# Seven half products for eight, in two phases, for the first FFN of six prompt tiles

## The chip, the cores and the metric

The kernel runs on one core of a Trainium2 chip. The metric is the device time of one execution in microseconds (us). Times of single instructions are in nanoseconds or microseconds as the profile gives them. An engine's name stands for its instruction stream: PE is the matrix engine, PEld its weight loads, DVE the vector engine, ACT the scalar engine, POOL is GpSimd, SP issues most DMAs.

## The reference, cut to what matters

One encoder layer is applied with the same weights to a prompt of 1024 tokens and a sample of 256 tokens of width 1024, all in float32:

```python
x = layer_norm(ALPHA * x + 0.5 * swiglu_1(x))          # the first FFN
x = layer_norm(ALPHA * x + mixing(x))                  # S5 and Hyena heads
x = layer_norm(ALPHA * x + 0.5 * swiglu_2(x))          # the second FFN
swiglu(x) = (silu(x @ w_gate) * (x @ w_up)) @ w_down   # 1024 -> 2816 -> 1024
```

## The kernel before

**Precision.** A float32 operand is split into a high and a low half in a reduced float32 type (`split`, L171 and L172: ACT writes the high half, DVE the difference). A product is three matmuls: high by high, high by low, low by high.

**Tiles.** Tokens come in tiles of 128: eight of the prompt, two of the sample. The hidden width of 2816 is cut into 22 columns of 128, each a "pass" `ft` below. The first FFN runs as two generators. `fa` has both sample tiles and prompt tiles 0 and 1. `fb` has prompt tiles 2 to 7, that is 768 tokens, held as chunks of 512 and 256 columns.

**fb before.** `ffn` transposes the tiles (L221) and then, for each pass, makes gate and up (`gate_up`, L298): 8 blocks of the width, 3 matmuls, 2 chunks, 2 matrices, which is 96 matmuls, half of them 512 and half 256 columns wide. After every two passes `down` (L331) multiplies the hidden values by `w_down` and adds to the residual rows (L336, L338). Gate/up of the next pass always stands ahead of the down products, so the two kinds alternate for the whole of `fb`. Hidden values stay in SBUF.

**What runs beside it.** `weave` takes a step of the generator that is furthest behind its share. While `fb` runs, `prep` is woven in. It prepares the S5 scan: `s5_prep` and the tables of `s5_mats` (`cmul`, L421 to L426) and then the matrices of `s5_mats` (L543 on DVE, short matmuls L611 and L623). A `yield` tells how much a step counts for, and the second number in `weave` is the generator's whole weight. The scheduler of the framework then orders each engine's instructions by when they become ready, and by the order in which they were written where several are; on the chip each engine runs its list in order.

**The second FFN of the prompt** already has the other form, at 1024 tokens. `Blocks` keeps the transposed tokens as seven blocks (four sums of them made on POOL, L1292, transposed in `put`, L1305). `GateUp` holds the weights of a pass and their four sums (DVE, L1348). `gated` makes gate and up for two token halves of 512 columns by seven products of 12 matmuls (L1368) instead of eight, combines them on DVE (L1384, L1425, L1433), and writes the hidden values to DRAM. When all 22 passes are done, `Down` reads them back with `w_down` and makes the down products (L1511) in groups of four passes.

Of the kernel before, what the change touches and what calls it, by code (L numbers as in the profile page):

```python
# [13 lines left out]
ALU = mybir.AluOpType  # L14
# [239 lines left out]
def ffn(K, NT, x, xT, wg, wu, wd, lng, lnb, cfg, done):  # L254
# [103 lines left out]
    for n, grp in enumerate(groups):  # L358
        last = n == len(groups) - 1
        for f in grp:  # L360
            if f not in hs:
                hs[f] = gate_up(f)
                yield unit
        if last:
            xT.free()
            wgu.free()
            lnv.append(K.new(2, D))
            load_row(K, lnv[0].v[:, 0], lng)
            load_row(K, lnv[0].v[:, 1], lnb)
        ws = [wdown(f) for f in grp]  # L370
        if last and "tail" in cfg:
# [6 lines left out]
    for b in [lnv[0], rawd, wdn, tmp] + hr + extras:  # L378
        b.free()
# [895 lines left out]
class Blocks:  # L1275
# [5 lines left out]
    def __init__(self, K):  # L1281
        self.K = K
        self.b = {n: (K.newr(4, 512), K.newr(4, 512)) for n in self.NAMES}
        self.tmp = K.ring(1, 4, 512)

    def even(self, a, j, banks):
        for n, c in (("11", 0), ("21", 512)):
            self.put(n, a[:, c:c + 512], j, banks)

    def sums(self, x):  # L1290

        TT = lambda o, a, b: self.K.nc.gpsimd.tensor_tensor(out=o, in0=a, in1=b, op=ALU.subtract)  # L1292
        t = self.tmp.get()
        a2, b1, b2 = x[:, 0, 512:1024], x[:, 1, 0:512], x[:, 1, 512:1024]
        TT(t[:, 0], b1, x[:, 0, 0:512])
        TT(t[:, 1], b2, t[:, 0])
        TT(t[:, 2], b2, b1)
        TT(t[:, 3], a2, t[:, 1])
        return {"22": b2, "t1": t[:, 0], "t2": t[:, 1], "t3": t[:, 2], "t4": t[:, 3]}
# [13 lines left out]
class GateUp:  # L1313
# [6 lines left out]
    def __init__(self, K, wg, wu):  # L1320
        self.K, self.wgu = K, (wg, wu)
        self.raw, self.bufs, self.w = {}, {}, {}
        self.sv, self.loaded = None, 0
# [9 lines left out]

    def parts(self, ft):
        K = self.K
        self.bufs[ft] = bg, bu = K.newr(2, 8, 128), K.newr(2, 4, 128)
        g, u = (self.raw[ft].v[:, i] for i in range(2))
        split(K, g, bg.v[:, 0], bg.v[:, 1])
        split(K, u[:, 4:8], bu.v[:, 0], bu.v[:, 1])
        self.w[ft] = {"g1": bg.v[:, :, 0:4], "g2": bg.v[:, :, 4:8], "u2": bu.v}  # L1340

    def sums(self, ft, second):

        K = self.K
        self.sv = self.sv or K.new(2, 4, 128)
        s = self.sv.v
        g, u = (self.raw[ft].v[:, i] for i in range(2))
        TT = lambda o, a, b, op: K.nc.vector.tensor_tensor(out=o, in0=a, in1=b, op=op)  # L1348
        if second:
            TT(s[:, 0], g[:, 4:8], s[:, 1], ALU.subtract)  # L1350
            TT(s[:, 1], g[:, 0:4], u[:, 0:4], ALU.subtract)
            self.raw.pop(ft).free()
        else:
            self.bufs[ft] += (K.newr(4, 4, 128), K.newr(4, 4, 128))
            TT(s[:, 0], u[:, 0:4], u[:, 4:8], ALU.add)
            TT(s[:, 1], s[:, 0], g[:, 0:4], ALU.subtract)
        b, o = [b.v for b in self.bufs[ft][2:]], 2 * second
        split(K, s, *(v[:, o:o + 2] for v in b))
        for i, n in enumerate((("s1", "s2"), ("s4", "s3"))[second]):
            self.w[ft][n] = [v[:, o + i] for v in b]  # L1360

    def product(self, ft, n, X, ps, first):
        a, b = self.OPS[n]
        w, x = self.w[ft][a], [p.v for p in X.b[b]]
        w = (w[:, 0], w[:, 1]) if a in ("g1", "g2", "u2") else w
        todo = [(d, i, k) for d in range(4) for i, k in ((0, 0), (0, 1), (1, 0))]
        for m, (d, i, k) in enumerate(todo):
            self.K.nc.tensor.matmul(ps, lhsT=w[i][:, d], rhs=x[k][:, d], start=first and m == 0, stop=m == len(todo) - 1,  # L1368
                                    skip_group_check=True)

    def free(self, ft):
        for b in self.bufs.pop(ft):
            b.free()
        self.w.pop(ft)


def gated(K, X, G, hd, ids, begin, spare):
# [5 lines left out]
    tmp, hb = K.ring(4, 512), K.ring(1, 2, 512)  # L1383
# [9 lines left out]
    def p1(ft):  # L1393
        st[ft] = s = {"ps": [K.ps[:, b * 512:b * 512 + 512] for b in ids[ft % 2]], "c1": tmp.get()}
# [48 lines left out]
    p7(0)  # L1443
    for ft in range(NFT):
# [6 lines left out]
        nc.sync.dma_start(out=hd[ft], in_=st.pop(ft)["h"].rearrange("p a t -> p (a t)"))  # L1451
        if ft < END:
# [11 lines left out]
    for r in (tmp, hb, G.sv):  # L1464
        r.free()


class Down:
# [24 lines left out]
    def run(self, x, lng, lnb, ids, done, cut):  # L1493
        K, nc = self.K, self.K.nc
        banks = Banks(K, ids)
        for g, grp in enumerate(self.GROUPS):
# [7 lines left out]
            for s in range(8):  # L1504
                o = s % 2 * 512 + s // 2 * 128
                for dh in range(2):
                    ps = banks.get(512)
                    todo = [(f, a, b) for f in grp for a, b in ((0, 0), (0, 1), (1, 0))]
                    for m, (f, a, b) in enumerate(todo):
                        p = self.p[f]  # L1510
                        nc.tensor.matmul(ps, lhsT=p[a].v[:, 1, o:o + 128], rhs=p[b].v[:, 0, dh * 512:dh * 512 + 512],  # L1511
# [40 lines left out]
def emit(ctx, tc, nc, A, dbg=None):  # L1552
# [5 lines left out]
              "rate": (2048,), "h": (NFT, 128, 1024), "x2": (128, 8, D)}  # L1558
# [76 lines left out]
    fb = ffn1([("prompt", s) for s in range(2, 8)], dict(bg=(0, 1, 2, 3), bd=(4, 5), tail=to_mix, rawd=2), turn1)  # L1635
# [10 lines left out]
    weave((fb, 33), (prep((6, 7)), 165))  # L1646
# [52 lines left out]
    class HyenaSide:  # L1699
# [42 lines left out]
        def prompt(self, ids, ids2, G):  # L1742
# [18 lines left out]
            def turn(j):  # L1761
                X.even(x[j].v[:, 0], j, tb)
                for n, v in X.sums(x[j].v).items():
                    X.put(n, v, j, tb)
                x.pop(j).free()

            for j in range(4):
                for i in range(2):
# [70 lines left out]
    dn = Down(K, g("ffn2_w_down"), scr["h"])  # L1839
# [12 lines left out]
    gated(K, X, G, scr["h"], ((0, 1, 2), (3, 4, 5)), begin, spare)  # L1852
# [5 lines left out]
    dn.run(xr[0], g("ln3_g"), g("ln3_b"), range(8), lambda s: nc.sync.dma_start(out=dst[:, s], in_=xr[0].at(s)), cut)  # L1858
# [32 lines left out]
```

## Time and profile before

| | us |
|---|---|
| median of 3 runs | 2580.35 (2579.68 to 2580.8) |
| the profiled execution, its own time | 2577.73 |
| its span, first to last instruction | 2575.9 |
| `fb`, from its first gate product to the last stretch before its tail | about 515 to 1085 of the span |
| second FFN of the prompt, gate/up in steady state | about 1930 to 2290 of the span |

A row "L338 DVE ... x24 | 16.4, 690 | 14.5" means: line 338 of the kernel, engine, 24 instructions, 16.4 us busy in total, 690 ns each on average, and 14.5 us of idle time of that engine just ahead of them. Durations of neighbours on one engine can overlap a little, so busy time is somewhat under count times mean.

### The profile page before, as it was taken

The page shows a single profiled execution, that of the slowest core. Times are in us where ns is not written, and L with a number is a line of the kernel's source. Part 1 is how long each engine was busy: PE and PEld are TensorE (multiplying, and loading weights), DVE is VectorE, ACT ScalarE, POOL GpSimd, SP SyncE. Part 2 cuts the span into 40 slices and gives each one's busy share as a digit, 9 for nine tenths or more (in the row PEclk, how much of TensorE's full clock was granted, in tenths as well). Part 3 has the DMA queues.
Part 4 walks back from the last instruction along what each step waited for, and adds up shares of the span by engine and source line. Part 5 has one row for each costly group of instructions (what it writes and reads, how often), then busy time and mean ns, then how long its engine had stood idle before and what let it go on. Part 6 is the DMA issues. An engine that isn't in the chain of part 4 may idle for free.

```text
span 2575.9 us, 32676 instructions
## 1 busy us (share of the span) xinstructions
PE 2516.0 (98%) x12833; PEld 2106.8 (82%) x12833; DVE 1809.3 (70%) x3016; ACT 812.6 (32%) x1218; POOL 74.7 (3%) x58
## 2 busy tenths in 40 slices
PE   8999999999999999999999999999989999999998
PEld 6767888888888888887888878998768888887887
DVE  7777777668944666558896788788986566556437
ACT  5443444321222222223444313333333222223200
POOL 0000000000000000000000000000230000000001
PEclk9999999999999999999999999999999999999999
DMA  6322333443522333355656654554433223244311
GB/s 202 120 86 85 100 106 104 164 111 112 164 81 75 108 108 98 97 147 147 177 171 193 224 196 144 171 185 148 156 107 98 74 82 91 74 156 179 127 37 66
DMA packets 329073, 326.44 MB, mean 127 GB/s; under 512 B 41068, under 2 KB 285445, under 8 KB 328150
## 3 DMA queue, kind: packets, MB, share of 16 engines
q1 hardware_dynamic: 293366, 305.99, 37.7%
q10 hardware_dynamic: 35552, 18.36, 2.7%
q8 instruction: 101, 1.65, 0.3%
q14 instruction: 54, 0.44, 0.1%
HBM read 249.57 MB, written 74.46 MB: 126 GB/s over the span
## 4 chain that ended last, share of the span: by engine, by line
PE 81%; DVE 12%; DMA 3%; issue 2%; POOL 1%; ACT 1%; SPq 0%; DVEq 0%; ACTq 0%; POOLq 0%
PE banks L298 25%; PE banks L1368 16%; PE banks L331 12%; PE banks L1511 8%; PE banks L857 4%; DVE s L927 3%; PE banks L774 3%; PE banks L1239 3%; PE banks L1061 2%; DVE s L172 2%; DMA s<-in_ffn_w_gate_dram 1%; PE banks L1202 1%; PE banks L1122 1%; DVE s L245 1%; DVE s L975 1%
## 5 line engine op out<-in xcount | busy, mean ns | idle before, releaser
L298 PE MATMUL banks<-s,s 128*128 128x512 f32 (+1 forms) x4224 | 789.8, 341 | 2.6 <-ACT s L171 1.6
L298 PEld LDWEIGHTS banks<-s,s 128*128 128x128 f32 x4224 | 648.3, 190 | 97.8 <-issue 10.3
L171 ACT ACTIVATE s<-s 128x1024 fp32r<-128x1024 f32 (+3 forms) x467 | 438.1, 956 | 859.2 <-PE banks L298 234.3
L172 DVE TENSOR_TENSOR s<-s,s 128x1024 fp32r<-128x1024 f32 (+3 forms) x467 | 504.8, 1095 | 190.4 <-ACT s L171 188.5
L1368 PE MATMUL banks<-s,s 128*128 128x512 f32 x1848 | 423.5, 391 | 4.4 <-DVE s L172 4.1
L1368 PEld LDWEIGHTS banks<-s,s 128*128 128x128 f32 x1848 | 347.6, 188 | 78.3 <-DVE s L172 5.1
L331 PE MATMUL banks<-s,s 128*128 128x512 f32 x1584 | 393.6, 396 | 2.4 <-ACT s L171 1.0
L331 PEld LDWEIGHTS banks<-s,s 128*128 128x128 f32 x1584 | 291.5, 189 | 64.3 <-issue 2.1
L857 PE MATMUL banks<-s,s 128*128 128x512 f32 (+1 forms) x1152 | 237.6, 360 | 0.0
L1511 PE MATMUL banks<-s,s 128*128 128x512 f32 x704 | 216.9, 389 | 1.8 <-DVE s L172 1.8
L857 PEld LDWEIGHTS banks<-s,s 128*128 128x128 f32 x1152 | 188.0, 189 | 27.9 <-DVE s L172 0.4
L338 DVE TENSOR_TENSOR s<-banks,s 128x512 f32<-128x512 f32 x204 | 138.9, 687 | 49.5 <-PE banks L331 48.4
L1511 PEld LDWEIGHTS banks<-s,s 128*128 128x128 f32 x704 | 132.1, 188 | 29.6 <-DVE s L172 2.1
L1384 DVE TENSOR_TENSOR s<-banks,s 128x512 f32<-128x512 f32 x110 | 75.9, 690 | 106.5 <-PE banks L1368 105.7
L1511 PE MATMUL banks<-s 128*128 128x512 f32 x352 | 137.0, 389 | 0.0
L1239 PE MATMUL banks<-s,s 128*128 128x512 f32 x480 | 122.5, 402 | 3.3 <-ACT s L171 1.5
L1517 DVE TENSOR_TENSOR s<-banks,s 128x512 f32<-128x512 f32 x80 | 54.9, 690 | 97.1 <-PE banks L1511 97.1
L230 POOL TENSOR_TENSOR cst<-cst 128x1 f32<-128x1 f32 (+2 forms) x38 | 50.0, 1315 | 2489.3 <-DVE cst L229 2485.2
L307 DVE SCALAR_TENSOR_TENSOR s<-banks,s 128x512 f32<-128x512 f32 (+1 forms) x88 | 47.5, 553 | 84.9 <-PE banks L298 84.1
L1239 PEld LDWEIGHTS banks<-s,s 128*128 128x128 f32 x480 | 88.1, 188 | 22.6 <-ACT s L171 2.0
L543 DVE TENSOR_TENSOR s<-s,cst 128x288 f32<-128x288 f32 (+1 forms) x128 | 53.5, 437 | 53.6 <-PE banks L623 27.0
L676 DVE TENSOR_TENSOR s<-banks,s 128x512 f32<-128x512 f32 (+2 forms) x112 | 59.2, 551 | 44.3 <-ACT s L793 20.4
(210 smaller groups left out, 2342.6 us busy)
## 6 DMA issues: line engine op xcount, KB each, us to landing
s<-in_ffn_w_down_dram SPq DMA_DIRECT2D x88, 512.0 KB
s<-in_ffn_w_gate_dram SPq DMA_DIRECT2D x66, 512.0 KB
s<-in_ffn_w_up_dram SPq DMA_DIRECT2D x66, 512.0 KB
s<-in_ffn_w_gate_dram SPq DMA_DIRECT2D x11, 1024.0 KB
s<-in_ffn_w_up_dram SPq DMA_DIRECT2D x11, 1024.0 KB
scr_h<-s SPq DMA_DIRECT2D x22, 512.0 KB
s<-scr_h SPq DMA_DIRECT2D x22, 512.0 KB
scr_tab<-s ACTq DMA_DIRECT2D x64, 160.0 KB
```

What stands on the lines that cost most here:

```text
L171: K.nc.scalar.activation(out=hi, in_=src, func=AF.Copy)
L172: K.nc.vector.tensor_tensor(out=lo, in0=src, in1=hi.bitcast(F32), op=ALU.subtract)
L298: nc.tensor.matmul(pss[-1][c], lhsT=w[:, wv, d], rhs=xT.parts[k][c].at(d), start=(d == 0 and wv == 0 and k == 0), stop=(d == 7 and wv == 1))
L331: nc.tensor.matmul(ps, lhsT=h[s // 4][:, a, s % 4 * 128:(s % 4 + 1) * 128], rhs=w[:, b, dh * 512:(dh + 1) * 512], start=(n == 0), stop=(n ...
L338: nc.vector.tensor_tensor(out=xv, in0=ps, in1=xv, op=ALU.add)
L774: nc.tensor.matmul(ps, lhsT=F[kt][a].v[:, s, i], rhs=b.v[:, s], start=(n == 0), stop=(n == 3 * NT // R - 1))
L857: nc.tensor.matmul(p, lhsT=w[:, wv, d], rhs=xT[nm].parts[k][c].at(d), start=(d == 0 and wv == 0 and k == 0), stop=(d == 7 and wv == 1))
L927: TT = lambda o, a, b, op: V.tensor_tensor(out=o, in0=a, in1=b, op=op)
L1239: nc.tensor.matmul(ps, lhsT=y[s // per][a].v[:, k, ts], rhs=W[k].v[:, b, dh * 512:dh * 512 + 512], start=(k == 0 and a == 0 and b == 0), s ...
L1368: self.K.nc.tensor.matmul(ps, lhsT=w[i][:, d], rhs=x[k][:, d], start=first and m == 0, stop=m == len(todo) - 1, skip_group_check=True)
L1384: TT = lambda o, a, b: V.tensor_tensor(out=o, in0=a, in1=b, op=ALU.add)
L1511: nc.tensor.matmul(ps, lhsT=p[a].v[:, 1, o:o + 128], rhs=p[b].v[:, 0, dh * 512:dh * 512 + 512], start=m == 0, stop=m == len(todo) - 1)
```

## The change

`fb` becomes `ffn1_halves`, which uses `Blocks`, `GateUp`, `gated` and `Down` on two halves of 384 columns (three tiles each). The hidden values go through a DRAM scratch `h1`. The four weight sums of a pass are made on GpSimd (`eng = K.nc.gpsimd if self.fine`), where the second FFN makes them on DVE. `fine` also gives each of the seven weight operands its own pair of 512-word buffers, freed as soon as its product is issued, and splits each by itself. The token sums are made in place (`tmp=False`). `gated` and `Down.run` become generators with yields of 0.6 and 0.4 per pass and 0.094 per pass and tile; the weight of `fb` in `weave` goes from 33 to 30. In the last group of `ffn` the rings `rawd` and `tmp` are freed earlier.

```diff
     def sums(self, ft, second):
-        self.sv = self.sv or K.new(2, 4, 128)
+        self.sv = self.sv or [K.new(4, 128) for _ in range(2)] if self.fine else self.sv or [K.new(2, 4, 128)]
...
-        TT = lambda o, a, b, op: K.nc.vector.tensor_tensor(out=o, in0=a, in1=b, op=op)
+        eng = K.nc.gpsimd if self.fine else K.nc.vector
+        TT = lambda o, a, b, op: eng.tensor_tensor(out=o, in0=a, in1=b, op=op)
         if second:
...
+            TT(s[0], g[:, 4:8], s[1], ALU.subtract)
+            TT(s[1], g[:, 0:4], u[:, 0:4], ALU.subtract)
             self.raw.pop(ft).free()
         else:
...
+            TT(s[0], u[:, 0:4], u[:, 4:8], ALU.add)
+            TT(s[1], s[0], g[:, 0:4], ALU.subtract)
...
+        if self.fine:
+            for n, v in zip(names, s):
+                self.put(ft, n, v)
+            return
...
-    fb = ffn1([("prompt", s) for s in range(2, 8)], dict(bg=(0, 1, 2, 3), bd=(4, 5), tail=to_mix, rawd=2), turn1)
+    def ffn1_halves(N, first, tail, turn):
+
+        tb, src = Banks(K, (6, 7)), tokens(A["x_prompt"][0], "prompt")
+        X = Blocks(K, N // 2, False)
+        for j in range(N // 2):
+            x = K.new(2, D)
+            for i in range(2):
+                nc.sync.dma_start(out=x.v[:, i], in_=src[:, first + 2 * j + i])
+            X.even(x.v, j, tb)
+            if j < N // 2 - 1:
+                X.odd(x.v, j, tb)
+                x.free()
+        G = GateUp(K, g("ffn1_w_gate"), g("ffn1_w_up"), True)
+        G.load()
+        yield 0.01
+        G.parts(0)
+        G.sums(0, 0)
+        G.sums(0, 1)
+        G.load()
...
+        dn = Down(K, g("ffn1_w_down"), scr["h1"], N)
...
+        yield from gated(K, X, G, scr["h1"], ((0, 1, 2), (3, 4, 5)), begin, spare)
...
+        yield from dn.run(xr[0], g("ln1_g"), g("ln1_b"), range(6), done, tail=tail)
+        xr[0].free()
+
+    fb = ffn1_halves(6, 2, to_mix, turn1)
...
-    weave((fb, 33), (prep((6, 7)), 165))
+    weave((fb, 30), (prep((6, 7)), 165))
```

In `Blocks`, the token sums and their transposes are now interleaved (`odd`), for the second FFN too.

## Rows read from the trace of the kernel before

**Rows 1.** The page's first part: busy time, share of the span and count of each engine.

```profile
PE 2516.0 (98%) x12833; PEld 2106.8 (82%) x12833; DVE 1809.3 (70%) x3016; ACT 812.6 (32%) x1218; POOL 74.7 (3%) x58
```

**Rows 2.** Busy time of each engine in stretches: the whole of `fb`; its first part, with `s5_prep` and the S5 tables; a part without `prep`; the part with the S5 matrices; the second FFN's gate/up in steady state; its start; the change to its down products. Columns: stretch, length, busy time and count by engine (PE, PEld, DVE, ACT, POOL), granted TensorE clock, DMA share, GB/s.

```profile
515.00:1085.00 570.00, 567.16 (x3079) 483.49 (x3078) 371.51 (x997) 138.04 (x266) 6.02 (x4) 1.00 0.37 105
515.00:720.00 205.00, 204.92 (x1093) 174.42 (x1092) 166.25 (x617) 50.58 (x93) 4.57 (x3) 1.00 0.46 127
720.00:800.00 80.00, 80.00 (x415) 68.31 (x414) 33.09 (x46) 14.04 (x22) 0.00 (x0) 1.00 0.28 85
800.00:1070.00 270.00, 270.00 (x1521) 230.84 (x1520) 161.22 (x314) 71.17 (x148) 0.00 (x0) 1.00 0.31 91
1930.00:2290.00 360.00, 360.00 (x1590) 298.09 (x1589) 216.02 (x287) 103.93 (x134) 0.00 (x0) 1.00 0.26 81
1880.00:1915.00 35.00, 26.57 (x120) 20.32 (x119) 31.38 (x43) 13.21 (x20) 16.17 (x11) 0.85 0.36 113
2320.00:2330.00 10.00, 8.17 (x35) 6.10 (x34) 7.67 (x7) 6.58 (x5) 0.00 (x0) 1.00 0.59 226
```

**Rows 3.** The same for L298 alone (gate/up products, both widths in equal number), PE and PEld, in the stretch without `prep`.

```profile
720.00:800.00 80.00, 47.79 (x271) 41.48 (x270) 1.00 0.28 85
```

**Rows 4.** The same for L331 alone (down products), in all of `fb` and in the stretch without `prep`.

```profile
515.00:1085.00 570.00, 175.95 (x736) 135.51 (x735) 1.00 0.37 105
720.00:800.00 80.00, 33.51 (x144) 26.84 (x144) 1.00 0.28 85
```

**Rows 5.** Transposes of `fb`'s tokens between products, PE in order of time: start, length, instruction, count.

```profile
500.57 0.60 PE L221 MATMUL banks<-cst,s 128*128 128x128 f32 x4
500.92 1.41 PE L331 MATMUL banks<-s,s 128*128 128x512 f32 x5
```

**Rows 6.** Groups of DVE instructions by shape in the second FFN's gate/up, 1930 to 2290 us: one shape of each kind.

```profile
L172 DVE TENSOR_TENSOR s<-s,s 128x1024 fp32r<-128x1024 f32 x57 | 69.8, 1226 | 49.0 <-ACT s L171 49.0
L1384 DVE TENSOR_TENSOR s<-banks,s 128x512 f32<-128x512 f32 x95 | 65.6, 690 | 93.7 <-PE banks L1368 93.0
L1348 DVE TENSOR_TENSOR s<-s,s 128x512 f32<-128x512 f32 x39 | 26.9, 689 | 0.7
...
L172 DVE TENSOR_TENSOR s<-s,s 128x512 fp32r<-128x512 f32 x19 | 13.0, 683 | 0.0
```

**Rows 7.** Groups of DVE instructions by shape, 720 to 800 us: one of 256 columns.

```profile
L307 DVE SCALAR_TENSOR_TENSOR s<-banks,s 128x256 f32<-128x256 f32 x3 | 1.2, 416 | 0.0
```

**Rows 8.** Groups of DVE instructions by line, 515 to 720 us: those that belong to the FFN.

```profile
L172 DVE TENSOR_TENSOR s<-s,s 128x1024 fp32r<-128x1024 f32 (+2 forms) x40 | 36.8, 950 | 10.9 <-ACT s L171 10.9
L338 DVE TENSOR_TENSOR s<-banks,s 128x512 f32<-128x512 f32 x29 | 19.7, 687 | 0.7 <-PE banks L331 0.4
...
L307 DVE SCALAR_TENSOR_TENSOR s<-banks,s 128x512 f32<-128x512 f32 (+1 forms) x16 | 8.2, 550 | 20.0 <-PE banks L298 20.0
L336 DVE SCALAR_TENSOR_TENSOR s<-s,banks 128x512 f32<-128x512 f32 x12 | 8.2, 685 | 0.9 <-PE banks L331 0.7
...
L245 DVE SCALAR_TENSOR_TENSOR s<-s,cst,s 128x1024 f32<-128x1024 f32 x4 | 5.1, 1278 | 0.4 <-POOL cst L230 0.4
L244 DVE SCALAR_TENSOR_TENSOR s<-s,cst,s 128x1024 f32<-128x1024 f32 x3 | 3.8, 1275 | 0.0
L239 DVE BATCH_NORM_STATS2 cst<-s 128x6 f32<-128x512 f32 x5 | 3.3, 685 | 0.0
```

**Rows 9.** The same for 800 to 1070 us.

```profile
L172 DVE TENSOR_TENSOR s<-s,s 128x1024 fp32r<-128x1024 f32 (+2 forms) x51 | 48.3, 958 | 22.4 <-ACT s L171 22.4
L338 DVE TENSOR_TENSOR s<-banks,s 128x512 f32<-128x512 f32 x48 | 33.0, 689 | 15.2 <-PE banks L331 14.9
...
L307 DVE SCALAR_TENSOR_TENSOR s<-banks,s 128x512 f32<-128x512 f32 (+1 forms) x20 | 10.7, 553 | 12.8 <-PE banks L298 12.3
```

**Rows 10.** Groups of POOL instructions by shape, 1840 to 1915 us: the token sums of the second FFN, the only element-wise sums on POOL in the kernel.

```profile
L1292 POOL TENSOR_TENSOR s<-s,s 128x512 f32<-128x512 f32 x8 | 14.0, 1750 | 0.3
L1292 POOL TENSOR_TENSOR s<-s 128x512 f32<-128x512 f32 x8 | 10.9, 1384 | 6.8 <-DVE s L245 6.8
```

**Rows 11.** POOL in order of time, while the last four of these sums run.

```profile
1903.30 3.28 POOL L1292 TENSOR_TENSOR s<-s 128x512 f32<-128x512 f32 x2 [2.06 <-DVE s L245]
1906.54 3.44 POOL L1292 TENSOR_TENSOR s<-s,s 128x512 f32<-128x512 f32 x2
```

**Rows 12.** DVE in order of time in the same stretch. "s" is an operand in SBUF, "banks" one in PSUM.

```profile
1903.08 0.68 DVE L172 TENSOR_TENSOR s<-s,s 128x512 fp32r<-128x512 f32 x1
1903.68 1.77 DVE L1348 TENSOR_TENSOR s<-s 128x512 f32<-128x512 f32 x1
1905.37 1.76 DVE L172 TENSOR_TENSOR s<-s,s 128x512 fp32r<-128x512 f32 x1
1907.05 1.77 DVE L1348 TENSOR_TENSOR s<-s,s 128x512 f32<-128x512 f32 x1
1908.74 0.68 DVE L172 TENSOR_TENSOR s<-banks,s 128x512 fp32r<-128x512 f32 x1
```

**Rows 13.** DVE in order of time during the eight sums before those, 1868 to 1890 us: the two instructions of L244 that are longer than the 1.28 us of the others.

```profile
1871.66 1.43 DVE L244 SCALAR_TENSOR_TENSOR s<-s,cst,s 128x1024 f32<-128x1024 f32 x1
...
1886.33 1.92 DVE L244 SCALAR_TENSOR_TENSOR s<-s,cst,s 128x1024 f32<-128x1024 f32 x1
```

**Rows 14.** Who waited for whom on PE at the start of the second FFN's gate/up, 1880 to 1915 us: waiting line, what it waited for, us in total, times, longest.

```profile
PE banks L1368 <- DVE s L172: 4.1, 3, 2.6
```

More of the change, by code (lines that the diff above doesn't have):

```diff
@@ L370, in ffn @@
         ws = [wdown(f) for f in grp]
+        if last:
+            rawd.free()
+            tmp.free()
         if last and "tail" in cfg:
@@ L1279, with __init__, even, odd @@
     NAMES = ("11", "21", "22", "t1", "t2", "t3", "t4")
[L1281 to L1286, printed above, removed]
-        for n, c in (("11", 0), ("21", 512)):
[L1288 to L1299, printed above, removed]
+    def __init__(self, K, pairs, tmp):
+        self.K, self.pairs, self.width = K, pairs, 128 * pairs
+        self.b = {n: (K.newr(4, self.width), K.newr(4, self.width)) for n in self.NAMES}
+        self.tmp = K.ring(1, 4, 512) if tmp else None
+    def even(self, x, j, banks):
+        for n, c in (("11", 0), ("21", 512)):
+            self.put(n, x[:, 0, c:c + 512], j, banks)
+    def odd(self, x, j, banks):
+        a1, a2, b1, b2 = (x[:, i, c:c + 512] for i in range(2) for c in (0, 512))
+        t = self.tmp.get() if self.tmp else None
+        t1, t2, t3, t4 = (t[:, i] for i in range(4)) if self.tmp else (a1, b2, b1, a2)
+        self.put("22", b2, j, banks)
+        for n, o, p, q in (("t1", t1, b1, a1), ("t3", t3, b2, b1), ("t2", t2, b2, t1), ("t4", t4, a2, t2)):
+            self.K.nc.gpsimd.tensor_tensor(out=o, in0=p, in1=q, op=ALU.subtract)
+            self.put(n, o, j, banks)
     def put(self, name, src, j, banks):
@@ L1356, in sums @@
[L1356 to L1359, printed above, removed]
+            TT(s[0], u[:, 0:4], u[:, 4:8], ALU.add)
+            TT(s[1], s[0], g[:, 0:4], ALU.subtract)
+        names = (("s1", "s2"), ("s4", "s3"))[second]
+        if self.fine:
+            for n, v in zip(names, s):
+                self.put(ft, n, v)
+            return
@@ L1360, in sums @@
+        if not second:
+            self.bufs[ft]["s"] = [K.newr(4, 4, 128), K.newr(4, 4, 128)]
+        b, o = [b.v for b in self.bufs[ft]["s"]], 2 * second
+        split(K, self.sv[0].v, *(v[:, o:o + 2] for v in b))
+        for i, n in enumerate(names):
             self.w[ft][n] = [v[:, o + i] for v in b]
@@ L1369, in product @@
                                     skip_group_check=True)
+        if self.fine:
+            for b in self.bufs[ft].pop(a):
+                b.free()
     def free(self, ft):
-        for b in self.bufs.pop(ft):
-            b.free()
+        for bufs in self.bufs.pop(ft).values():
+            for b in bufs:
+                b.free()
         self.w.pop(ft)
@@ L1463, in gated @@
             p7(ft + 1)
-    for r in (tmp, hb, G.sv):
+            yield 0.6
+    for r in [tmp, hb] + G.sv:
         r.free()
@@ L1761, in turn @@
             def turn(j):
-                X.even(x[j].v[:, 0], j, tb)
-                for n, v in X.sums(x[j].v).items():
-                    X.put(n, v, j, tb)
+                X.even(x[j].v, j, tb)
+                X.odd(x[j].v, j, tb)
                 x.pop(j).free()
```

98 lines of the change are left out of this document (60 added, 38 removed).

## The prediction

> **What bounds the kernel now.** I read the page's first part first: PE is busy 98% of the span, DVE 70%, POOL 3% [rows 1]. So time is saved by giving PE less to stream, as long as nothing else becomes slower than PE. Next, the busy time by stretches: in all of `fb` (515 to 1085 us) PE stands still for 2.8 of 570 us [rows 2]. DVE is busy for 371.5 of 570 there, but unevenly: 166 of 205 us (81%) in the part with the S5 tables, 33 of 80 (41%) where `prep` does nothing. The reader is to see two things: `fb` is bound by PE now, and its first part has little DVE time to give away. Then I read the second FFN, which already has the new form: PE has no gap from 1930 to 2290 us, with DVE at 216 of 360 [rows 2]. There is no `prep` beside it.
>
> **The products.** One 512-column matmul costs 360 us / 1590 = 0.2264 us, taken from the uniform stretch [rows 2]. In the 80 us without `prep`, 144 down products take 144 x 0.2264 = 32.6 us [rows 4]; the other 47.4 us hold 271 gate/up products [rows 3], half of each width, so a pair of 512 and 256 columns costs 0.350 us and the 256 one 0.123. Before: 22 x 96 = 2112 products, 1056 pairs, 369 us. After: 22 x 7 x 12 = 1848 products of 384 columns. The trace has no such width. Half way between the two widths gives 0.175 us, 323 us in all; three quarters of the 512 price gives 0.170, 314 us. I take 319, a gain of 50 us, with 46 and 56 as ends. The down products (22 x 36 of 512 columns) stay.
>
> **More on PE.** Seven blocks of three pairs of tiles need 84 transposes of 128x128, where six tiles needed 48: nine groups of four more. A group holds PE for 0.35 us [rows 5]. That is 3 us.
>
> **The start.** `begin`, the first splits and the first sums stand between `fa` and the first pass. At the second FFN's start PE was busy for 26.6 of 35 us, at a granted clock of 0.85 (it had idled before and in it) [rows 2], and the longest waits were for DVE's splits [rows 14]: 8.4 us of idle time and 35 x 0.15 = 5 us of clock. In `fb` as it is the start costs next to nothing, because `fa`'s last down products cover it. They will cover part again, so I take 8 us, between 0 and 13.
>
> **Between the phases.** The hidden values are read back before the first down product. Where the second FFN does this, PE is busy for 8.2 of 10 us [rows 2]. I take 2 us, bounds 0 and 4. The DMA traffic of 22 hidden columns out and back is 17 MB over some 540 us, 32 GB/s on top of 105 [rows 2]; the second FFN's turn bears 226, so no term. The loads of weights wait in SP's list behind the write of the pass before, as they do in the second FFN, where no PE time is lost to it. ACT has 104 of 360 us there [rows 2] and gets no term.
>
> **DVE in phase one.** This is the step that decides. In the second FFN a pass lasts 84 x 0.2264 = 19.0 us, of which DVE is busy for 216/360, 11.4 us [rows 2]. For the new pass I subtract four weight sums, 4 x 0.689 = 2.8 us [rows 6]; add the difference between seven splits of 512 words (7 x 0.683 = 4.78) and three of 1024 and one of 512 (3 x 1.226 + 0.683 = 4.36), 0.4; and take off the narrowing of seven instructions from 512 to 384 columns, from 0.690 to half way to 0.416, which is 0.553, so 1.0 us [rows 6, 7]. That leaves 8.1 us a pass, 178 in 22 passes.
>
> `prep` comes on top. In 515 to 720 us DVE was busy for 166.3 us, of which the FFN's lines make 85.1 [rows 8], so 81 are `s5_prep` and the tables. In 800 to 1070 it is 161.2 less 92.0 [rows 9], so 69 for the matrices. By the yields, `prep` counts 28 + 56 + 64 = 148 of its weight of 165, and phase one takes `fb` to 22 of 30, so `prep` to 121: all of the first two and 37 of the last 64. So 81 + 0.58 x 69 = 121 us of `prep` are in phase one. DVE has 178 + 121 = 299 us to do.
>
> PE has 319 us plus `prep`'s short matmuls. Of the 570 us, 369 + 736 x 0.2264 = 536 are products [rows 4], 2.8 idle, and the other 31 are transposes, short matmuls and the tail; I put 10 into phase one: 329 us. So DVE alone would just fit, at 91%.
>
> **POOL's sums on DVE's time.** There are 88 weight sums of 128x512. The trace has only 16 such sums on POOL [rows 10], at 1.29 us when undisturbed, 1.75 on average in one form. POOL itself has time: 7 us of a 14.5 us pass at that average. But while the last four run [rows 11], DVE's instructions with two operands in SBUF take 1.77 us for 0.69, and the one that reads PSUM takes its 0.68 [rows 12]. So one such sum can cost DVE 1.08 us. Of the eight sums before, only two instructions are stretched, by 0.15 and 0.64 us [rows 13], and the other four stretch none: all 16 together cost DVE 3 x 1.08 + 0.79 = 4.0 us, 0.25 each. Those earlier sums met mostly DVE instructions that read PSUM or one operand. In the new pass nine of 14 instructions, and all of `prep`'s sums, have two operands in SBUF. So the bounds are 0.25 and 1.08 us a sum, 22 and 95 us in 88. The last four (0.81 on average) are the nearest row, but the five PSUM additions of each pass give POOL some free slots: I take 0.65, 57 us. DVE then needs 299 + 57 = 356 us against PE's 329, and PE waits 27 us, with 0 and 65 as ends. What is late next are PE's own operands: the products of the next pass wait for DVE's splits, and `prep` stands in DVE's list between them.
>
> The Trainium skill says the same more sharply. "SBUF — State Buffer", section "Who interferes with whom", says that a DVE instruction with two SBUF inputs and a GpSimd instruction that reads SBUF exclude each other for the whole instruction. The trace agrees, with 1.77 us for 0.69, and also shows that a PSUM operand escapes. By that rule alone each sum would hold DVE for its full 1.29 us: 114 us in all, a wait of 84 and not 27, and a sum below of +47.
>
> **The sum.** -50 (products) + 3 (transposes) + 8 (start) + 2 (turn) + 27 (DVE) = -10 us. The profiled execution took 2577.7 us, 2.6 less than the median of the runs: 2567.7 there, 2570 as a median.
>
> **The rivals.**
> *DVE keeps up.* POOL's sums fall into DVE's free time or beside its PSUM instructions (22 us, so 321 of 329), or the scheduler pushes `prep` into phase two, where DVE has time. For it: PE had no gap in 515 to 720 with DVE at 81%. Then -50 + 13 = -37: 2543, or 2538 with the larger gain. Chance 0.24.
> *DVE is the bound of phase one*, the other sign. Every sum costs its 1.08 us, because `prep` fills whatever DVE time is free: 394 us of DVE against 329, 65 us of waiting, -50 + 13 + 65 = +28: 2608. It decides from a wait of 37 us on. For it: rows 12, and that DVE has nearly no free time left in phase one. Against it: the other 12 sums cost little. Chance 0.30.
> *The start is dear.* The token sums (12 of them) and the first eight weight sums stand on POOL one behind the other, 20 x 1.3 = 26 us, while DVE still does `fa`'s norms. If PE waits out the whole of that instead of 8 us, the sum is +8: 2588. `fa`'s last down products speak against it. Chance 0.06.
> The forecast itself, a gain mostly given back, has 0.40.
>
> **How the numbers follow.** About 0.2%, 5 us, is what a measurement of this kernel can tell from no change. The forecast's own range is 2555 to 2585, so of its 0.40 some 0.27 are faster, 0.11 the same and 0.02 slower. The second case adds 0.24 to faster; the third 0.30 to slower; the start 0.02 to the same and 0.04 to slower. Faster 0.51, same 0.13, slower 0.36. The range goes from the larger gain of the second case, 2538, to the middle of the third, 2608, and leaves out some 0.2: half of the third case and a little below.
>
> **What would show it.** L298 disappears from `fb` and 1848 products at L1368's place take 0.170 to 0.175 us each where PE has no gaps. In phase one PE is idle for some 27 us, ended by DVE's splits (L172) and additions. DVE is busy over 90% of the first 12 or so passes, its two-operand instructions in SBUF show means well over 0.69 us for 512 words, and POOL has 88 sums of 1.3 to 1.8 us. Phase two has no gaps. The prediction is wrong if PE is full in phase one (then POOL's sums cost less than 0.34 us each: 30 us of room), or if its idle time is over 37 us; and the step on the products is wrong if a 384-column matmul costs more than 0.18 us without waits.

## The result, and the profile after

The changed kernel takes 2612.32 us (median of four runs, 2608.8 to 2616.03) against 2580.01 us (2579.45 to 2580.8) for the kernel before on the same chip: a ratio of 1.0125, interval 1.0108 to 1.0143. It is 32 us slower. The forecast was 2570 us, range 2538 to 2608: the sign is wrong, and the time lies just above the range. The profiled execution took 2612.26 us, its span 2610.5 for 2575.9 before. One execution of experiment 9's kernel took 3058 us at a granted clock of 0.75, where its others have 0.99; medians and ranges leave it out.

The page's first part for the kernel after, against [rows 1]:

```profile
span 2610.5 us, 32833 instructions
...
PE 2499.4 (96%) x12605; PEld 2124.7 (81%) x12605; DVE 1934.4 (74%) x3153; ACT 865.8 (33%) x1315; POOL 213.3 (8%) x158
```

PE is busy for 17 us less than before and stands still for longer: 111 us of the span instead of 60. DVE is busier by 125 us, although the 88 weight sums of the new form are POOL's. The reader should ask at once what these 125 us are. (In experiment 1 below, which has the 88 sums on DVE for 60 us, it is busy for 1919.5 us: so 50 of the 125 are the new form's own work, and 75 came with POOL's sums.)

Stretches of the kernel after, against [rows 2]: the start of phase one (gate and up), the rest of it, phase two (down), and two slices of phase one, early and late. Columns as there.

```profile
527.00:551.00 24.00, 15.99 (x76) 13.88 (x74) 23.04 (x37) 8.87 (x16) 15.19 (x10) 0.86 0.77 221
551.00:942.00 391.00, 347.32 (x1922) 335.26 (x1923) 343.55 (x891) 138.21 (x286) 114.60 (x82) 0.96 0.46 132
942.00:1141.00 199.00, 197.33 (x941) 161.50 (x940) 146.47 (x236) 49.90 (x69) 7.54 (x5) 1.00 0.48 146
560.00:580.00 20.00, 16.33 (x81) 16.01 (x80) 19.68 (x71) 5.51 (x12) 5.22 (x4) 0.83 0.42 60
820.00:840.00 20.00, 20.00 (x120) 19.64 (x119) 14.37 (x25) 7.28 (x17) 7.84 (x6) 1.00 0.40 111
```

Most of the loss is in phase one (25.0 of 34.6 us, see the balance), and it is plainest where DVE is full: in the slice at 560 us DVE is busy for 19.7 of 20 us, PE stands still for 3.7 us and the granted clock has fallen to 0.83. At 820 us, beside a lighter part of `prep`, PE has no gap at all. Phase two has next to none.

The waits of PE, then of DVE, then of ACT in phase one of the kernel after (who waited, for whom, us in total, times, longest):

```profile
PE banks L1388 <- DVE s L1409: 28.3, 13, 4.0
PE banks L614 <- DVE s L546: 6.6, 4, 2.3
PE banks L1388 <- DVE s L172: 5.5, 3, 2.9
PE banks L1308 <- DVE s L172: 5.1, 2, 4.3
```

```profile
DVE s L172 <- ACT s L171: 24.2, 21, 3.3
```

```profile
ACT s L171 <- POOL s L1363: 104.5, 49, 5.6
```

L1388 are the products (L1368 before), L1409 the additions out of PSUM in `gated`, L171 and L172 the two halves of a split, L1363 the weight sums on POOL, L614 and L546 belong to `prep`. PE waits for DVE's PSUM additions above all: 13 waits of 2.2 us. DVE, for its part, waits 21 times for ACT's half of a split; in 14 of them (16.0 of the 24.2 us) ACT had just waited for POOL's sum.

**The balance.** From `fa`'s end to the first matmul of the mixing stage the span has 614.2 us, where it had 589.2: +25.0. The terms: products -50 (1848 of them at a median of 173 ns from start to start are 319.7 us, for the 369 that the rows of before gave); transposes +1.8 (20 of the 84 stand in phase one, five groups of 0.35 us [rows 5]; 64 come before `fa` ends, where before it was all 48); idle time of PE in phase one 51.6 us, of which 8.0 before 551 us is the start and 43.6 the rest; and clock. In seven places the granted clock is 0.50 (1.2 of 2.4 GHz), 37.5 us in all, each in or just after a wait of PE of 1.8 to 4.4 us; not every such wait brings it, one of 3.2 us at 739 us did not. Half of that is 18.8 us; 2.4 of them fall on time in which PE waits anyway, so 16.3 us are lost work. -50 + 1.8 + 51.6 + 16.3 = +19.7, for 25.0: some 5 us are in none of these terms, and no run separates them. The other 9.6 us of the span's +34.6 lie outside: `fa` ends 2.7 us later (the four groups of transposes that it has more make 1.4 by estimate); from the mixing stage to the first product of the second FFN it takes 7.7 us longer (at this FFN's start the clock costs a busy PE 8.3 us for 3.9); and what follows is 0.9 us shorter.

### The profile page after: what moved, and what is told of

Same layout as the page of the kernel before. It is cut to its first block, busy times and chain, and to the rows that moved or that the text cites. A ratio compares the mean times of both kernels' runs of the same rounds, so it can differ in the third digit from the quotient of the medians.

```text
span 2610.5 us, 32833 instructions
## 1 busy us (share of the span) xinstructions
PE 2499.4 (96%) x12605; PEld 2124.7 (81%) x12605; DVE 1934.4 (74%) x3153; ACT 865.8 (33%) x1315; POOL 213.3 (8%) x158
## 4 chain that ended last, share of the span: by engine, by line
PE 68%; DVE 20%; DMA 4%; issue 3%; POOL 2%; ACT 2%; SPq 0%; ACTq 0%; DVEq 0%; POOLq 0%
PE banks L1388 19%; PE banks L1541 14%; PE banks L298 12%; PE banks L331 5%; DVE s L172 4%; PE banks L860 4%; DVE s L930 3%; PE banks L777 3%; PE banks L1242 3%; PE banks L1064 2%; POOL s L1363 1%; ACT s L171 1%; DVE s L245 1%; DMA s<-in_ffn_w_gate_dram 1%; DVE s L1409 1%
## 5 line engine op out<-in xcount | busy, mean ns | idle before, releaser
L1388 PE MATMUL banks<-s,s 128*128 128x512 f32 (+1 forms) x3500 | 768.7, 371 | 26.2 <-DVE s L1409 17.0
L171 ACT ACTIVATE s<-s 128x1024 fp32r<-128x1024 f32 (+4 forms) x533 | 478.9, 915 | 845.5 <-PE banks L1541 132.9
L1388 PEld LDWEIGHTS banks<-s,s 128*128 128x128 f32 x3500 | 647.0, 191 | 106.4 <-DVE s L1409 19.2
L172 DVE TENSOR_TENSOR s<-s,s 128x1024 fp32r<-128x1024 f32 (+4 forms) x533 | 570.1, 1081 | 181.4 <-ACT s L171 170.0
L298 PE MATMUL banks<-s,s 128*128 128x512 f32 (+1 forms) x2112 | 400.5, 342 | 2.4 <-ACT s L171 1.2
L1541 PE MATMUL banks<-s,s 128*128 128x512 f32 x1232 | 386.8, 392 | 0.1
L298 PEld LDWEIGHTS banks<-s,s 128*128 128x128 f32 x2112 | 325.4, 191 | 53.0 <-issue 10.3
L1541 PEld LDWEIGHTS banks<-s,s 128*128 128x128 f32 x1232 | 230.4, 188 | 46.6 <-DVE s L172 0.6
L1541 PE MATMUL banks<-s 128*128 128x512 f32 x616 | 241.2, 392 | 0.0
L860 PE MATMUL banks<-s,s 128*128 128x512 f32 (+1 forms) x1152 | 237.6, 360 | 0.0
L1409 DVE TENSOR_TENSOR s<-banks,s 128x384 f32<-128x384 f32 (+1 forms) x220 | 136.0, 618 | 111.9 <-PE banks L1388 110.9
L860 PEld LDWEIGHTS banks<-s,s 128*128 128x128 f32 x1152 | 188.3, 189 | 28.2 <-DVE s L172 0.4
L331 PE MATMUL banks<-s,s 128*128 128x512 f32 x792 | 200.8, 396 | 4.1 <-ACT s L171 2.3
L1547 DVE TENSOR_TENSOR s<-banks,s 128x512 f32<-128x512 f32 x140 | 95.8, 688 | 134.3 <-PE banks L1541 134.2
L331 PEld LDWEIGHTS banks<-s,s 128*128 128x128 f32 x792 | 144.9, 188 | 35.7 <-ACT s L171 2.7
L1541 PEld LDWEIGHTS banks<-s 128*128 128x128 f32 x616 | 115.8, 188 | 22.7
L1242 PE MATMUL banks<-s,s 128*128 128x512 f32 x480 | 124.7, 407 | 4.1 <-ACT s L171 1.6
L1242 PEld LDWEIGHTS banks<-s,s 128*128 128x128 f32 x480 | 89.3, 190 | 23.4 <-ACT s L171 2.0
L171 ACT ACTIVATE s<-banks 128x512 fp32r<-128x512 f32 x81 | 46.8, 596 | 131.1 <-PE banks L221 68.0
L777 PE MATMUL banks<-s,s 128*128 128x256 f32 x624 | 89.7, 285 | 0.0
```

What stands on the lines that cost most here:

```text
L171: K.nc.scalar.activation(out=hi, in_=src, func=AF.Copy)
L172: K.nc.vector.tensor_tensor(out=lo, in0=src, in1=hi.bitcast(F32), op=ALU.subtract)
L298: nc.tensor.matmul(pss[-1][c], lhsT=w[:, wv, d], rhs=xT.parts[k][c].at(d), start=(d == 0 and wv == 0 and k == 0), stop=(d == 7 and wv == 1))
L331: nc.tensor.matmul(ps, lhsT=h[s // 4][:, a, s % 4 * 128:(s % 4 + 1) * 128], rhs=w[:, b, dh * 512:(dh + 1) * 512], start=(n == 0), stop=(n ...
L777: nc.tensor.matmul(ps, lhsT=F[kt][a].v[:, s, i], rhs=b.v[:, s], start=(n == 0), stop=(n == 3 * NT // R - 1))
L860: nc.tensor.matmul(p, lhsT=w[:, wv, d], rhs=xT[nm].parts[k][c].at(d), start=(d == 0 and wv == 0 and k == 0), stop=(d == 7 and wv == 1))
```

## The experiments

Three theories are weighed against each other. *The port*: a POOL sum that reads SBUF shuts DVE's two-operand instructions out while it runs. *The load*: DVE simply has too much to do beside `prep`, on whichever engine the sums are. *Late sums*: DVE's list stands at a split whose sum POOL has not finished. Four kernels leave work out or add idle work (`e2_no_sums`, `e5_unread_sums`, `e6_memsets`, `e9_paced_memsets`): in `fb` they multiply by raw halves of the weights in place of the weight sums. The others compute everything.

**1. The sums back on DVE.**

```diff
-        eng = K.nc.gpsimd if self.fine else K.nc.vector
+        eng = K.nc.vector
```

> The changed kernel with the weight sums of fb on DVE, the rest unchanged. Theory A (POOL's sums hold DVE up: in the trace of the changed kernel DVE instructions of phase one are stretched by some 70 us in all): DVE gets 88 x 0.61 = 54 us of work and is rid of 70 us of stretching, so its load is about the same, and the scheduler now sees it; PE idles 30 to 50 us in fb and the time is 2595 to 2612. Theory B (DVE simply has too much to do beside prep, POOL's sums cost it nothing): 54 us more on the engine that is the bound, 2645 to 2665.

Measured: 2566.86 us (2564.6 to 2575.05), ratio to the kernel before 0.995 (0.9935 to 0.9966). With 60 us more work in its list DVE lets phase one end 47 us earlier (367.7 us for 415.0), PE's idle time falls from 51.6 to 17.4 us and the lost clock from 16.3 to 3.9. The time is below what either theory had said (2595 at the least): the sums cost far more on POOL than they do on DVE. The load alone can't be the cause. But it is not free: DVE is 95% busy.

**2. No sums.**

```diff
-        if second:
+        if self.fine:
+            s = [g[:, 4:8], u[:, 0:4]] if second else [u[:, 0:4], u[:, 4:8]]
+        elif second:
...
```

> The four weight sums of a pass are left out, and the raw halves of the weights go into the splits in their place: no work on POOL, the same splits, products and DMAs. Theory A: DVE is rid of the stretching and has its 299 us for 329, PE idles under 20 us in fb, of which some 8 at the start, and the time is 2540 to 2560. Theory B: PE idles as before, over 40 us, and the time is 2600 to 2615.

Measured: 2549.43 us (2546.57 to 2554.67), ratio 0.9883 (0.9864 to 0.9903). Phase one takes 351.1 us with 7.6 idle. So the price of making the sums is 63 us on POOL and 17 on DVE.

**3. The sums made by POOL, but read by nobody.** This is experiment 2 with

```diff
...
+            if second:
+                TT(s[0], g[:, 4:8], g[:, 0:4], ALU.subtract)
+                TT(s[1], g[:, 0:4], u[:, 0:4], ALU.subtract)
+            else:
+                TT(s[0], u[:, 0:4], u[:, 4:8], ALU.add)
+                TT(s[1], u[:, 0:4], g[:, 0:4], ALU.subtract)
...
```

> As without sums (the raw halves go into the splits, so the output is not the layer's), but POOL makes 88 sums of the same shape from the same raw weights, and nothing reads them. Nothing waits for POOL but the next load into the raw buffer. Port (a POOL sum shuts DVE's instructions with two SBUF operands out while it runs): stretching of DVE as in the changed kernel, 50 us or more, idle PE over 25 us, 2580 to 2605. Lateness (the loss comes from sums that arrive late and from what stands behind them in ACT's and DVE's lists): as without sums, 2545 to 2557.

Measured: 2634.07 us (2628.07 to 2642.22), ratio 1.0215 (1.0192 to 1.0238). No instruction needs a sum, and the kernel is 85 us slower than without them, slower even than the changed kernel and than the 2605 that the port theory had for its end. What does wait for POOL here is the next load into the weights' buffer, but ACT stands waiting for such loads no longer than in experiment 2 (11.5 us for 14.6). So a loss of this size needs no late sum.

**4. and 5. POOL as busy, but only writing.** Experiment 2 with eight memsets of 128x512 for each pass in place of the sums. In the first of the two they follow no input and in the second they write onto buffers whose splits must be done:

```diff
...
+            for b in s:
+                eng.memset(b, 1.0)
+                eng.memset(b, 1.0)
...
```

```diff
...
                 self.put(ft, n, v)
+            for v in s + s:
+                eng.memset(v, 1.0)
...
```

> As without sums, with 88 POOL instructions of 128x512 that only write (memsets into the sums' buffers, unread; the output is again not the layer's). Port, by what a sum reads: no stretching, 2545 to 2557. If any POOL work on SBUF costs DVE time: over 2565.

> As without sums (output not the layer's), with 176 memsets on POOL, each on a half of the raw weights just after its split has read it, so that POOL works all through phase one (92 us in all) and not in one burst. Port, by what the POOL instruction reads: DVE's sums and differences are not stretched, 2547 to 2560, but for single DVE copies. Any POOL work stretches DVE: over 2575.

Measured, the second: 2556.45 us (2550.97 to 2561.2), ratio 0.991 (0.989 to 0.993). POOL is busy for 92 us with 176 memsets and phase one takes 355.9 us, 5 more than with nothing on POOL. The first (also 176 memsets, not the 88 that its expectation names) took 2561 us once and 2603 to 2617 three times, so no ratio is given and it decides nothing here; its profiled run, of 2603 us, has one wait of PE of 43.2 us, told in the last section.

Phase one of the kernel after and of experiments 1, 2, 3 and 5 (columns as in [rows 2]):

```profile
527.00:942.00 415.00, 363.31 (x1998) 349.14 (x1997) 366.59 (x927) 147.08 (x302) 129.79 (x92) 0.95 0.48 137
530.00:898.00 368.00, 350.56 (x1994) 337.92 (x1994) 350.63 (x1010) 148.54 (x301) 5.72 (x4) 0.99 0.54 154
529.00:880.00 351.00, 343.37 (x1997) 336.61 (x1995) 306.62 (x921) 147.01 (x298) 5.64 (x4) 0.99 0.57 163
528.00:965.00 437.00, 369.39 (x2000) 356.14 (x1999) 389.26 (x926) 147.99 (x299) 141.47 (x92) 0.93 0.46 131
528.00:883.00 355.00, 344.35 (x1994) 335.56 (x1993) 308.47 (x925) 147.33 (x299) 96.98 (x180) 0.99 0.56 160
```

Four of these kernels in one view, the groups of DVE and POOL instructions by shape from 530 to 880 us (between the bars: busy us, mean ns of one). The kernel after:

```profile
L172 DVE TENSOR_TENSOR s<-s,s 128x512 fp32r<-128x512 f32 x138 | 109.8, 813 | 24.8 <-ACT s L171 24.2
L1409 DVE TENSOR_TENSOR s<-banks,s 128x384 f32<-128x384 f32 x91 | 49.8, 547 | 2.1 <-PE banks L1388 2.0
...
L1363 POOL TENSOR_TENSOR s<-s 128x512 f32<-128x512 f32 x40 | 56.7, 1418 | 27.0 <-DVE s L172 19.7 <-DVE s L425 1.7 <-DMA s<-in_ffn_w_up_dram 1.6
```

Sums on DVE (experiment 1):

```profile
L172 DVE TENSOR_TENSOR s<-s,s 128x512 fp32r<-128x512 f32 x152 | 102.0, 689 | 4.7 <-ACT s L171 4.3
```

Unread sums on POOL (experiment 3):

```profile
L172 DVE TENSOR_TENSOR s<-s,s 128x512 fp32r<-128x512 f32 x134 | 119.1, 911 | 10.1 <-ACT s L171 10.0
...
L1363 POOL TENSOR_TENSOR s<-s 128x512 f32<-128x512 f32 x84 | 130.0, 1581 | 208.3 <-DMA s<-in_ffn_w_up_dram 206.9 <-DVE s L245 1.5
```

Paced memsets (experiment 5):

```profile
L172 DVE TENSOR_TENSOR s<-s,s 128x512 fp32r<-128x512 f32 x153 | 103.0, 691 | 20.0 <-ACT s L171 19.7
...
L1378 POOL MEMSET s<- 128x512 f32 x176 | 91.5, 528 | 234.6 <-DVE s L172 204.5 <-issue 12.5 <-DVE s L562 8.5
```

The split with two operands in SBUF takes 813 and 911 ns on average beside sums on POOL, 689 and 691 without them or beside memsets; L1409, which reads PSUM, keeps its 547. Over all shapes in phase one the time above the median that each shape has in experiment 2 is 61 us in the kernel after, 84 with unread sums and under 4 in experiments 1, 2 and 5. (By busy time, from first to last product: DVE's 366.5 us after stand against 350.3 less 60 of sums in experiment 1, so 76 us; with unread sums 389.2 against 306.9, so 82.) The port theory holds, with its price.

What it looks like from near, DVE and then POOL in order of time in the kernel after (start, length):

```profile
753.82 0.17 DVE L424 TENSOR_TENSOR s<-s 128x4 f32<-128x4 f32 x1
753.90 1.27 DVE L427 TENSOR_TENSOR s<-s 128x4 f32<-128x4 f32 x1
755.09 0.15 DVE L425 TENSOR_TENSOR s<-s,s 128x4 f32<-128x4 f32 x1
755.28 1.27 DVE L426 TENSOR_TENSOR s<-s,s 128x4 f32<-128x4 f32 x1
756.58 0.17 DVE L428 TENSOR_TENSOR s<-s,s 128x4 f32<-128x4 f32 x1
```

```profile
753.86 1.29 POOL L1363 TENSOR_TENSOR s<-s,s 128x512 f32<-128x512 f32 x1 [11.27 <-DVE s L554]
755.23 1.29 POOL L1363 TENSOR_TENSOR s<-s 128x512 f32<-128x512 f32 x1
```

A DVE sum of four words a partition, 0.16 us long, takes 1.27 when it comes 40 to 50 ns after a POOL sum has begun, and ends when that sum ends (755.17 and 755.15; 756.55 and 756.52). DVE's small sums of `prep` pay as much as its large ones. The Trainium skill says this of the pair, in "SBUF — State Buffer", section "Who interferes with whom": one excludes the other for the whole instruction, and a GpSimd instruction that only writes doesn't. The trace agrees with both halves, by 1.27 us for 0.16 and by the 691 ns beside memsets.

**6. Half of the sums on each engine.**

```diff
+        if second:
+            eng = K.nc.vector
```

> The changed kernel with the second two of a pass's four sums on DVE, the first two on POOL. Between 2612 (all on POOL) and 2567 (all on DVE). Port: half the stretching, about 27 us, 2585 to 2595. Lateness: the second two were at the end of the chain, so most of the loss goes, 2568 to 2578.

Measured: 2586.49 us (2584.63 to 2594.73), ratio 1.0032 (1.002 to 1.0044): between the kernel after and experiment 1, as are stretching (38 us), idle time (29.9) and lost clock (10.4).

**7. to 9. Another pace of `prep`.** Experiment 7 spreads `prep` more evenly over both phases, with the sums on POOL; experiment 8 does it with the sums on DVE; experiment 9 goes half of the way (a yield of 0.13 and a weight of 36).

```diff
-                yield len(grp) * 0.094
+                yield len(grp) * 0.188
...
-            if n in (1, 2, 5):
+            if n in (1, 2):
...
-    weave((fb, 30), (prep((6, 7)), 165))
+    weave((fb, 42), (prep((6, 7)), 165))
```

> Sums on POOL as in the changed kernel; the steps of phase two count double in the weave and fb's weight is 42, so that 86 and not 121 of prep's units are in phase one and the matrices (L546) fall into phase two; phase two keeps one column less read ahead, for space. Both theories: phase one is rid of some 40 us of DVE work, the idle time next to L546 (some 12 us, 850 to 906 us) goes, the tables' part stays as it is: 2590 to 2600. If the place of prep does not matter (the waits come from the order of the products alone), 2610.

> Both edits: the sums on DVE and the new pace. Theory A: phase one asks DVE for 178 + 54 + 81 = 313 us against PE's 329, no stretching: PE idles some 20 us in fb, 2550 to 2565, faster than before. Theory B: as slow as with the sums on DVE alone less the matrices' part, 2625 to 2650.

> All sums on DVE, and a pace between those tried: phase two's steps count 0.130, fb's weight is 36, one column less read ahead. If phase one's DVE load sets the time, between 2567 (0.094, 30) and 2558 (0.188, 42): 2558 to 2564. If it is all noise beyond the sums on DVE: 2560 to 2568.

Measured: on POOL 2613.51 us (2608.34 to 2615.82), ratio 1.0126 (1.0107 to 1.0146), the same as without the new pace. On DVE 2557.57 us (2550.96 to 2562.66), ratio 0.9904 (0.9879 to 0.9929), and 2563.57 us (2560.06 to 2565.38), 0.9938 (0.9921 to 0.9954), half way. PE's idle time in phase one is then 6.5 and 9.3 us. Every version with all weight sums on DVE (1, 8, 9 and 10) beats both kernels; 8 and 10 have the shortest times. With the sums on DVE what is left is load, and a lighter phase one is worth some 9 us (2566.9 to 2557.6). With the sums on POOL PE's idle time stays: 47.7 us after 51.6, though DVE's busy share falls from 0.88 to 0.83, where both theories had expected a gain of 12 to 22 us. So the sums on POOL do something that load doesn't describe.

**10. All sums on DVE**, the token sums too. This is experiment 8 with

```diff
-            self.K.nc.gpsimd.tensor_tensor(out=o, in0=p, in1=q, op=ALU.subtract)
+            (self.K.nc.gpsimd if self.tmp else self.K.nc.vector).tensor_tensor(out=o, in0=p, in1=q, op=ALU.subtract)
```

> The new pace and the weight sums on DVE, and fb's 12 token sums on DVE too: no sum of fb is on POOL. The start of phase one loses some of its 5 to 8 us of waiting, since nothing holds DVE there: 2550 to 2556. If DVE's work at the start is the bound anyway, 7 us of sums more on it: 2558 to 2566.

Measured: 2558.43 us (2556.47 to 2561.76), ratio 0.9916 (0.9899 to 0.9933), the same as experiment 8. Phase one is 2 us shorter, but begins 6 us later: the start's cost went into `fa`'s tail.

**11. No `prep` beside phase one**, with the sums on POOL:

```diff
-            if n in (1, 2, 5):
+            if n in (1, 2):
...
-    weave((fb, 30), (prep((6, 7)), 165))
+    steps(fb, 44)
+    weave((fb, 10), (prep((6, 7)), 165))
```

> Sums on POOL as in the changed kernel, but prep is woven in only after phase one (one column less read ahead). Phase two will be long; phase one is what is read. Port with a full DVE as the condition: DVE has 178 us of work and up to 95 of stretching in about 330, so phase one has under 15 us of idle PE, most at the start, and takes 330 to 340 us where the changed kernel's takes 415. If the waits come from late sums in the lists' order: 30 us of idle or more.

Measured: 2697.45 us (2695.65 to 2698.46), ratio 1.0457 (1.0441 to 1.0472). The whole is slower after phase one, where `prep` has moved: from 896 to 1250 us PE is busy for 258 of 354 us. What counts is phase one, its row and its waits:

```profile
530.00:896.00 366.00, 337.13 (x1875) 328.28 (x1874) 234.34 (x327) 130.10 (x226) 120.72 (x92) 0.98 0.36 111
```

```profile
PE banks L1388 <- DVE s L1409: 20.5, 21, 2.6
```

DVE is busy for 64% here and PE still waits 21 times in 22 passes, 1 us each, and stands still for 28.9 us in all. Phase one takes 365.9 us, where the port theory with a full DVE as its condition had 330 to 340 and under 15 of idle time, and late sums had 30 or more: a full DVE is not needed for the loss. One of the waits, DVE, POOL and PE in order of time:

```profile
700.74 1.22 DVE L172 TENSOR_TENSOR s<-s,s 128x512 fp32r<-128x512 f32 x1 [2.14 <-ACT s L171]
702.11 1.77 DVE L172 TENSOR_TENSOR s<-s,s 128x512 fp32r<-128x512 f32 x1
703.81 1.14 DVE L1409 TENSOR_TENSOR s<-banks,s 128x384 f32<-128x384 f32 x2
```

```profile
700.12 1.29 POOL L1363 TENSOR_TENSOR s<-s 128x512 f32<-128x512 f32 x1
702.04 1.30 POOL L1363 TENSOR_TENSOR s<-s 128x512 f32<-128x512 f32 x1 [0.63 <-DVE s L172]
```

```profile
704.41 0.45 PE L1388 MATMUL banks<-s 128*128 128x384 f32 x1 [0.84 <-DVE s L1409]
```

In a pass, product 7's bank must be read by DVE (L1409) before product 4 may write it, and only product 1 lies between: 12 x 0.173 = 2.1 us. Ahead of that addition in DVE's list stand two splits of 0.69 us each, and two things make them late. They begin late: DVE stands idle for 2.14 us before the first and 0.15 before the second, until POOL has made the sum and ACT its half. And they are held: beside POOL's next sums they take 1.22 and 1.77 us. So the addition begins at 703.81, and PE waits 0.84 us for it; without the 1.08 us that the second split is held the addition would have been in time. 20 of the 21 waits look like this. DVE has time, but the instruction that PE waits for stands behind ones that came late and were held, and this run does not separate the two.

**12. The other FFN.** In the kernel before, the second FFN's weight sums put on POOL:

```diff
-        TT = lambda o, a, b, op: K.nc.vector.tensor_tensor(out=o, in0=a, in1=b, op=op)
+        TT = lambda o, a, b, op: K.nc.gpsimd.tensor_tensor(out=o, in0=a, in1=b, op=op)
```

> The kernel before, with the weight sums of the second FFN on POOL and not on DVE; no prep runs there. Port with a full DVE as the condition: DVE has 8.7 us of work in a pass of 19 and up to 4.3 us of stretching, so PE does not wait in steady state and the time stays within 0.3% of before. If the order of the lists is what counts (one late sum holds up what stands behind it, however much free time DVE has): PE waits in every pass, 10 us or more in all.

Measured: 2588.32 us (2583.4 to 2590.66), ratio 1.0033 (1.0023 to 1.0044). The steady state and, below it, PE's waits at the start, to be read against [rows 2, 14]:

```profile
1960.00:2280.00 320.00, 320.00 (x1413) 265.00 (x1412) 155.92 (x184) 91.31 (x118) 94.14 (x68) 1.00 0.27 84
```

```profile
PE banks L1305 <- DVE s L172: 6.1, 3, 4.9
PE banks L1368 <- ACT s L171: 3.4, 1, 3.4
PE banks L1368 <- DVE s L172: 2.4, 1, 2.4
```

```profile
L172 DVE TENSOR_TENSOR s<-s,s 128x1024 fp32r<-128x1024 f32 x51 | 70.8, 1389 | 91.1 <-ACT s L171 91.1
```

Here POOL's sums cost PE nothing in steady state, although they stretch DVE's splits too (1389 ns for the 1226 of [rows 6]): DVE is half idle, and product 1 lasts 12 x 0.2264 = 2.7 us, not 2.1. What it costs is the start. So the sums on POOL and not on DVE cost 8 us in one FFN (2588.3 for 2579.9) and 45 in the other (2612.3 for 2566.9). The two differ in what stands beside them, and in their form too: wider products, and one split for two sums. As PE waits in experiment 11 without `prep`, `prep` alone doesn't make the difference.

## Why the prediction was wrong

**Products: right.** 1848 at a median of 173 ns, 319.7 us, for the forecast's 319. **Transposes: right**, 84 for 48, but only 20 of them in phase one. **Start: right** as idle time, 8.0 us for 8; the clock lost in it, 3.1 us where the working put 5 beside it, was left out of the 8. **Turn: too high**, no gap there for the forecast's 2.

**DVE's work: right.** The forecast put 299 us of DVE into phase one without stretching, and experiment 1 has 290 without its sums. Stretching: forecast 57 us, measured 61 to 76, so 0.69 to 0.87 us a sum for 0.65, inside the bounds of 0.25 and 1.08. POOL's sums take 1.26 to 2.28 us, 1.41 on average, where 1.3 to 1.8 was said.

**PE's work in phase one**: 329 us forecast, 347 measured (415.0 less 51.6 idle and 16.3 of clock). The forecast put 10 of 31 us of transposes and `prep`'s short matmuls into phase one; 27 lie there beside the products' 319.7.

**The wait for DVE: the step that failed.** "DVE then needs 299 + 57 = 356 us against PE's 329, and PE waits 27 us". Both totals were near, and with the measured ones, 366 and 347, this step would give 19 us. Measured are 43.6 us of waiting and 16.3 of clock on top, beside the 8.0 of the start. Phase one lasts 415 us where the fuller of the two engines has 366 to do. The step takes the length of a stretch for the larger of two sums. That is a lower bound. DVE itself stands still for 49 of the 415 us, while PE waits for additions further down its list. Late sums don't explain these 49 us by themselves: 16 us of DVE's waits stand behind one, but DVE also stands still for 48 us with unread sums and for 44 with none. The excess over the larger total is 49 us after, 48 with unread sums, 22 with half of the sums, 17 with the sums on DVE, 9 with none (there PE is the fuller one): in these five kernels it is larger where more is stretched.

**The clock: a term that was missing.** The forecast's bound for the start had 5 us, the rest of phase one nothing; 16.3 us were lost, and 4.4 more than before at the second FFN's start.

**The rivals.** "DVE is the bound of phase one" forecast 2608 and was 4 us off, on the right side. Its condition (a wait over 37 us) held, with 43.6; its reason only in part: a sum cost 0.69 to 0.87 us and not 1.08, DVE had 366 us to do and not 394, and the number was made up by waits beyond DVE's load and by the clock, which this rival did not have. That it came so near is in part luck. By the Trainium skill's rule alone the sum was +47, with 1.29 us a sum; measured are +34.6 of span, and not every sum meets an instruction that it can hold. "DVE keeps up" is what experiment 2 shows with the sums gone (2549 for its 2543). "The start is dear" did not come: 8 us.

**Left open.** How much of the 43.6 us is the order in DVE's list, with splits that come late or are held, and how much its load was not separated: experiment 11 shows about 1 us a pass without a full DVE, 20 of the 44, but there DVE's list has none of `prep` in it. Why `fa` ends later by the 1.3 us that its transposes don't explain was not tried either.

## What to carry over

Before moving an element-wise sum from VectorE to GpSimd, look at what VectorE does meanwhile: here each two-operand SBUF instruction that came while a sum ran was held until the sum ended, however short it was, so work that costs VectorE 0.69 us a sum (60 us for 88) cost it 0.69 to 0.87 us of holding and the kernel 45 us more. When the totals of two engines that feed each other come within a tenth, don't take the larger one as the time: find the instruction that the other engine waits for, count what stands ahead of it in its list, when that can begin, and how long the partner's work covers it. And add to TensorE's waits the clock that they cost: here some 50 us of them, in pieces of up to 4 us, brought a loss of 16 us at half clock.

## What the runs showed of the hardware beyond that

Memsets on POOL that wait for nothing (experiment 4) ran as one burst from 540 to 623 us. DVE in order of time, POOL beside it, and PE's longest wait:

```profile
575.81 0.68 DVE L172 TENSOR_TENSOR s<-s,s 128x512 fp32r<-128x512 f32 x1
...
577.02 46.10 DVE L487 COPY s<-s 64x128 f32<-64x128 f32 x1
577.16 45.97 DVE L1416 TENSOR_TENSOR s<-banks,s 128x384 f32<-128x384 f32 x1
...
623.48 0.69 DVE L510 TENSOR_SCALAR s<-s 64x1024 f32<-64x1024 f32 x1
```

```profile
576.31 0.99 POOL L1366 MEMSET s<- 128x512 f32 x2
577.25 0.99 POOL L1367 MEMSET s<- 128x512 f32 x2
```

```profile
PE banks L1395 <- DVE s L487: 43.2, 1, 43.2
```

Splits with two operands kept their 0.68 us beside the memsets. A copy of 128 words within SBUF, one operand, took 46.10 us: it came to an end only with the burst, and everything behind it in DVE's list stood. So it looks as if this copy was shut out by POOL's writes, which two-operand sums were not, and did not get its turn between memsets that follow each other at once. An equal copy at 569 us, in the same burst, took only 0.50 us. With the memsets spaced (experiment 5) the same copies took 0.28 us on average, for 0.21 with no memsets (experiment 2). This is one case in one trace; what decides the turn was not tried.
